# Holding the modulation steps of a two-layer RWKV/attention kernel behind VectorE's work on the tile in front, and ordering them by halves of c

## The chip, the cores and the metric

The kernel runs on one core of one Trainium2 chip. The metric is the device time of one execution in microseconds (us), the median of several runs. One further execution was taken with the hardware profiler; the views of the profile and of the trace quoted here are of that execution. TensorE is PE in them (PEld its weight loads), VectorE DVE, ScalarE ACT, GpSimd POOL, and SyncE, which issues most transfers, SP.

## The reference

A sequence of 256 positions with 2048 features passes an RWKV-7 layer and an attention layer, each followed by an MLP, all in fp32. Every normalised input is shifted and scaled, and every branch is gated, by vectors that come from one conditioning vector c ("modulation"):

```python
for layer in range(DEPTH):                      # DEPTH = 2
    mod = c @ w_ada[layer] + b_ada[layer]       # 2048 x 12288
    sh1, sc1, gt1, sh2, sc2, gt2 = jnp.split(mod, 6, axis=-1)
    if layer == N_A_LAYERS:
        sh_kv, sc_kv = jnp.split(c @ w_ada_kv + b_ada_kv, 2, axis=-1)
        h_kv = modulate(rms_norm(x, g_kv), sh_kv, sc_kv)
        k_s, v_s = h_kv @ w_k_shared, h_kv @ w_v_shared
    h = modulate(rms_norm(x, g_mix[layer]), sh1, sc1)
    y = rwkv7_time_mix(h, ...) if layer < N_A_LAYERS else chunk_band_attention(h, ...)
    x = x + gt1[:, None, :] * y
    h = modulate(rms_norm(x, g_mlp[layer]), sh2, sc2)
    x = x + gt2[:, None, :] * sq_relu_mlp(h, w_up[layer], w_down[layer])
return rms_norm(x, g_final)
```

## The kernel before, in words

The program passes these stages; the times are those of the trace of before.

| stage | us |
|---|---|
| first modulation vectors on TensorE, v projection | 0 to 190 |
| time mixing | 190 to 704 |
| out_proj with `w_o` | 704 to 797 |
| MLP 0: four quarters of 16 up tiles and 16 down tiles | 797 to 1556 |
| shared K (first 8 tiles to 1607, last 8 to 1653) | 1556 to 1653 |
| shared V: 16 tiles | 1653 to 1748 |
| q and the attention itself: 16 tiles | 1748 to 1882 |
| out_proj with `attn_w_o`: 16 tiles | 1882 to 1970 |
| MLP 1, as MLP 0 | 1970 to 2707 |

**A weight tile** comes in two halves of 128x1024. Each half is loaded into `raw` (six buffers, SP's queue), ScalarE rounds it to `wH` (L380), VectorE takes `wL = raw - wH` (L383), and TensorE multiplies by both parts (`proj2`, L414 and L415). There are three buffers of wH and wL, so TensorE has at most one and a half tiles ahead of it. VectorE then takes the result out of PSUM: `t`, `vf` or `q` at L934, `x` at L919 (the output projections) and L990 (the MLPs), and splits activations in two parts (`hHL` L965, `aHL` L543).

**A modulation step** handles one of 384 tiles of 512 KB of `w_ada_t`: VectorE multiplies the tile by a broadcast half of c (`cb`) and sums along the row (L461). A modulation vector ("key", such as (1, 4): layer 1, part 4) has 16 tiles for each half of c, 32 steps in all. Its two halves of sums are added at the end (L463 of the changed program, L466 to L469 of the one before), and the key is then in `ada_done`. The order is that of `ada_tiles`: key by key, both halves of a key in turn, the half that comes first alternating, so that c's half changes at every key's middle. `cb` has one buffer: a change waits for the last step with the old half, then loads 512 KB over SP. There are 13 such loads.

In the time mixing (steps 0 to 110) the tiles come through `raw`. Later they come through `rada` in an `ada_room`, by GpSimd's queue (L370): five buffers in MLP 0, three in the attention with its output projection, five in MLP 1. `ada_fill` asks for the next tiles as buffers come free. The program asks for steps 111 to 285 in MLP 0 (`ada_tick`: one and two by turns behind each tile), 286 to 293 in the second half of K (one a tile), 294 to 325 in V (two a tile), 326 to 347 beside q (one, and two at every third tile), 348 to 351 in the `ada_need` ahead of the attention's output projection (L610), 352 to 363 in that projection, and 364 to 383 in MLP 1. `ada_need` takes steps until the named keys are done: (1, 2) is the gate that the projection's x updates use, (1, 4) and (1, 3) are the scale and shift of the MLP behind it.

That is the order in which the program is written. A scheduler then orders the instructions of each engine by when their operands are ready, and may draw an instruction ahead of those written earlier, unless it is written in `tc.issue_after(instruction)`, which keeps it behind that instruction. The steps have no such mark.

Of the kernel before, what the change touches and what calls it, by code (L numbers as in the profile page):

```python
# [12 lines left out]
F32 = mybir.dt.float32  # L13
F32R = mybir.dt.float32r
AF = mybir.ActivationFunctionType
ALU = mybir.AluOpType
AX = mybir.AxisListType

P = 128
D = 2048  # L20
T = 256
KT = D // P
# [8 lines left out]
HK = 8  # L31
# [298 lines left out]
class Body:  # L330
# [96 lines left out]
        return tile_, self.bada[:, at:at + KT]  # L427

    def ada_tiles(self):
        for key in [(0, 2), (0, 4), (0, 3), (0, 5), ("kv", 1), ("kv", 0),  # L430
                    (1, 1), (1, 0), (1, 2), (1, 4), (1, 3), (1, 5)]:
            for last in range(2):
                for n in range(KT):
                    yield key, last, n

    def ada_load(self):
        tile_ = next(self.adas, None)
        if tile_ is not None:
            key, last, n = tile_
            if n == 0 and last:  # L440
                self.half = 1 - self.half
            raw = self.raw(self.d["w_ada_t"][self.ada_src(*key)[0] + n, self.half], ada=True)
            self.ada_q.append((key, last, n, raw))
        return tile_ is not None

    def c_half(self):
        n_ = HK * P
        self.cb = self.wp.tile([P, n_], F32, tag="cb", bufs=1, name="cb")
        self.nc.sync.dma_start(out=self.cb, in_=self.d["c_row"][0:1, self.cb_half * n_:(self.cb_half + 1) * n_].to_broadcast([P, n_]))
        self.cb_half = 1 - self.cb_half  # L450

    def ada_step(self):
        nc = self.nc
        if not (self.ada_q or self.ada_load()):
            return
        key, last, n, raw = self.ada_q.popleft()
        if self.cb is None:
            self.c_half()
        dst, bias = self.mods[key], self.ada_src(*key)[1]
        sums = dst if last else self.sums  # L460
        nc.vector.scalar_tensor_tensor(out=raw, in0=raw, scalar=1.0, in1=self.cb, op0=ALU.mult, op1=ALU.mult,  # L461
                                       accum_out=sums[:, n:n + 1])
        if n < KT - 1:  # L463
            return
        if last:
            nc.vector.tensor_tensor(out=dst, in0=dst, in1=self.sums, op=ALU.add)  # L466
            self.ada_done.add(key)
        else:
            nc.vector.tensor_tensor(out=self.sums, in0=self.sums, in1=bias, op=ALU.add)  # L469
            self.c_half()  # L470

    def ada_fill(self):
        while self.ada_pool and len(self.ada_q) < self.ada_pool[1] - 1 and self.ada_load():
# [5 lines left out]
            self.ada_step()  # L479

    def ada(self, n=1):
        for _ in range(n):
            self.ada_step()
        self.ada_fill()

    def last_pe(self):
        pe = self.nc.tensor.engine
        return next(i for i in reversed(self.nc.cur_bb.bb.instructions) if i.engine == pe)

    def ada_need(self, *keys):  # L490
        while not all(k in self.ada_done for k in keys):
# [74 lines left out]
    def run(self):  # L566
        nc, tc, d = self.nc, self.tc, self.d
        ctx = self.ctx
        gp = self.gp = ctx.enter_context(tc.tile_pool(name="gp", bufs=1))
        self.wp = ctx.enter_context(tc.tile_pool(name="wp", bufs=2))  # L570
        nc.scalar.preload_act_table_set("natural_log_exp_and_others")
        self.hp = ctx.enter_context(tc.tile_pool(name="hp", bufs=2))
        self.csts = gp.tile([P, CST.shape[1]], F32, name="csts")
        self.vecs = gp.tile([P, len(VECS), KT], F32, name="vecs")
        self.bada = gp.tile([P, 2 * 96 + 32], F32, name="bada")
        self.ct = gp.tile([P, KT], F32, name="ct")
        nc.scalar.dma_start(out=self.ct, in_=d["c"])
        self.mods = {}
        for layer in (0, 1, "kv"):
            for part in range(2 if layer == "kv" else 6):  # L580
                self.mods[(layer, part)] = gp.tile([P, KT], F32, name=f"mod_{layer}_{part}")
        self.nhalf, self.pool_every = 0, 0
        self.ada_pool, self.half, self.cb, self.cb_half = None, 0, None, 0
        self.sums = gp.tile([P, KT], F32, name="ada_sums")
        self.ada_done = set()
        self.adas, self.ada_q = self.ada_tiles(), deque()

        sv, sp = ExitStack(), ExitStack()
        v = self.layer_a(sv, sp)
        with ExitStack() as st:  # L590
            self.np = st.enter_context(tc.tile_pool(name="npl", bufs=1, side="right", reuse_waits="tile"))
            xp = st.enter_context(tc.tile_pool(name="xp", bufs=1, side="right", reuse_waits="tile"))
            self.x = xp.tile([P, KT, T], F32, name="x")
            for j in range(KT - 2, KT):
                self.split(self.y_hl, j, v[:, j, :])
            sv.close()
            self.ada_need((0, 2), (0, 4), (0, 3))
            nxt = self.out_proj(self.pp, "w_o", self.y_hl, (0, 2), "g_mlp0", (0, 4), (0, 3), self.o_ps)
            sp.close()
            with ExitStack() as s2:  # L600
                pp = s2.enter_context(tc.tile_pool(name="ps_m0", bufs=2, space=bass.MemoryType.PSUM, reuse_waits="tile"))
                self.psm = lambda: pp.tile([P, 512], F32, tag="m", bufs=2, name="m")
                s2.enter_context(self.ada_room(5))
                nxt = self.mlp(s2, pp, 0, *nxt, "g_kv", ("kv", 1), ("kv", 0))
            with ExitStack() as s2:
                pp = s2.enter_context(tc.tile_pool(name="ps_at", bufs=2, space=bass.MemoryType.PSUM, reuse_waits="tile"))
                self.psm = lambda: pp.tile([P, 512], F32, tag="m", bufs=1, name="m")
                s2.enter_context(self.ada_room(3))
                o_hl = self.attention(s2, pp, *nxt)
                self.ada_need((1, 2), (1, 4), (1, 3))  # L610
                nxt = self.out_proj(pp, "attn_w_o", o_hl, (1, 2), "g_mlp1", (1, 4), (1, 3))
            with ExitStack() as s2:
                pp = s2.enter_context(tc.tile_pool(name="ps_m1", bufs=2, space=bass.MemoryType.PSUM, reuse_waits="tile"))
                self.psm = lambda: pp.tile([P, 512], F32, tag="m", bufs=2, name="m")
                s2.enter_context(self.ada_room(5))
                self.mlp(s2, pp, 1, *nxt)
                r = self.rstd()
                for lo, hi, eng in ((0, 4, nc.vector), (11, 14, nc.gpsimd), (4, 8, nc.vector), (8, 11, nc.vector),
                                    (14, KT, nc.gpsimd)):
                    x = self.x[:, lo:hi, :]  # L620
                    eng.tensor_tensor(out=x, in0=x, in1=r.unsqueeze(1).to_broadcast([P, hi - lo, T]), op=ALU.mult)
                    (nc.sync if eng is nc.vector else nc.scalar).dma_start(out=d["out"][:, lo:hi, :], in_=x)
# [388 lines left out]
    def attention(self, st, pp, scaled, kv_gain, kv_shift):  # L1011
# [8 lines left out]
        def projected(src, hl, dst, ada, between=()):  # L1020

            between = iter(between)
            w = self.weight(src)
            ps = pp.tile([P, 2, T], F32, tag="pj", bufs=2, name="pj")
            for q in range(0, KT, 4):
                ins = self.proj2(ps, w, lambda kt: hl[:, kt, :, 0:T], (q, q + 4))
                with tc.issue_after(ins):
                    next(between, lambda: None)()
            self.sum2(dst, ps)
            self.ada(ada)  # L1030
# [171 lines left out]
```

## Time and profile before

| | us |
|---|---|
| runs | median of 3: 2716.94 (2716.22 to 2721.14) |
| profiled execution, device time | 2709.22 |
| its span in the profile | 2707.5 |
| PE busy | 2596.7 (96%) |
| VectorE busy | 2088.7 (77%) |
| ScalarE busy | 1334.1 (49%) |
| GpSimd busy | 350.2 (13%) |

In rows of the timeline the columns are start, duration, engine, line, operation, output<-input, shape, and in brackets the idle time ahead of it with what ended it. In rows of groups they are line, engine, operation, names, count, busy time and mean ns, idle time ahead with its releasers. In rows of waits: engine, tile and line, what it waited for, us in all, times, the longest. In rows of stretches: the stretch, its length, the busy time and count of each engine named in the text, the granted clock of TensorE, the DMA engines' share and GB/s. Consecutive VectorE instructions overlap a little, so a duration is slightly longer than the distance from start to start.

### The profile page before, as it was taken

To read this page: it belongs to the slowest core of one execution; us is meant where nothing else is said; L and a number is where in the kernel's file an instruction comes from. 1 tells how busy PE (TensorE), PEld (TensorE's weight loads), DVE (VectorE), ACT (ScalarE), POOL (GpSimd) and SP (SyncE) were. 2 spreads that over 40 slices of the span, in tenths; PEclk is the share of its full clock that TensorE was granted. 3 is DMA by queue.
4 is the path that set the end of the run, shared out by engine and by line. 5 is a ranking of instruction groups with operands and counts; after the bars stand their busy time and mean duration, and the time that the engine had idled before them with its cause. 6 is when DMAs were issued, how large, how long until landed. Compare 5 with 4: busy or idle time off the path is not lost.

```text
span 2707.5 us, 55672 instructions
## 1 busy us (share of the span) xinstructions
PE 2596.7 (96%) x22154; PEld 2215.5 (82%) x22154; DVE 2088.7 (77%) x3493; ACT 1334.1 (49%) x2432; POOL 350.2 (13%) x593
## 2 busy tenths in 40 slices
PE   6998999999999999999989999999999999999997
PEld 3777778777889888888877898877898888888886
DVE  5778888889699999999888884577985555555555
ACT  3345545555445445355345554465464464453553
POOL 0001322323121111121111100000200000000002
PEclk8999999999999999999999999999999999999998
DMA  9976656566698999999999655555855555555553
GB/s 334 314 236 210 201 187 199 192 200 225 236 323 307 370 365 380 383 382 357 354 349 336 231 197 184 184 172 196 289 190 188 187 189 186 188 187 187 188 187 117
DMA packets 219253, 669.28 MB, mean 247 GB/s; under 512 B 21616, under 2 KB 69104, under 8 KB 218992
## 3 DMA queue, kind: packets, MB, share of 16 engines
q1 hardware_dynamic: 173520, 516.36, 55.9%
q0 software_dynamic: 39312, 143.15, 14.4%
q10 hardware_dynamic: 6160, 6.21, 0.7%
q8 instruction: 174, 2.85, 0.4%
q14 instruction: 87, 0.71, 0.1%
HBM read 663.54 MB, written 2.10 MB: 246 GB/s over the span
## 4 chain that ended last, share of the span: by engine, by line
PE 63%; issue 13%; DVE 12%; DMA 6%; ACT 2%; POOL 2%; SPq 0%; DVEq 0%; POOLq 0%; ACTq 0%
PE pj L414 33%; PE pj L415 16%; DVE wL L383 4%; DMA raw<-w_ada_t 3%; DVE rada L461 2%; POOL rada L370 2%; DMA cb<-c_row 2%; PE pj L404 2%; PE pj L405 2%; PE pj L403 2%; DVE raw L461 1%; PE iv L111 1%; PE ms L324 1%; ACT wH L380 1%; DVE x L919 1%
## 5 line engine op out<-in xcount | busy, mean ns | idle before, releaser
L383 DVE TENSOR_TENSOR wL<-raw,wH 128x1024 fp32r<-128x1024 f32 x772 | 943.1, 1222 | 356.6 <-ACT wH L380 352.1
L414 PE MATMUL pj<-aHL,wH 128*128 128x512 f32 x3328 | 1207.9, 404 | 2.1 <-DVE x L919 1.2
L380 ACT CAST wH<-raw 128x1024 fp32r<-128x1024 f32 x772 | 803.7, 1043 | 720.8 <-PE pj L414 611.9
L415 PE MATMUL pj<-aHL,wL 128*128 128x256 f32 x3328 | 940.0, 282 | 16.6 <-DVE wL L383 15.9
L414 PEld LDWEIGHTS pj<-aHL,wH 128*128 128x128 f32 x3328 | 632.7, 190 | 156.1 <-issue 10.3
L414 PE MATMUL pj<-hHL,wH 128*128 128x512 f32 x2048 | 723.8, 399 | 4.1 <-DVE hHL L965 4.1
L415 PEld LDWEIGHTS pj<-aHL,wL 128*128 128x128 f32 x3328 | 632.6, 190 | 25.1 <-DVE wL L383 23.5
L415 PE MATMUL pj<-hHL,wL 128*128 128x256 f32 x2048 | 574.4, 281 | 5.7 <-DVE wL L383 5.7
L414 PEld LDWEIGHTS pj<-hHL,wH 128*128 128x128 f32 x2048 | 384.7, 188 | 100.4 <-DVE hHL L965 5.4
L415 PEld LDWEIGHTS pj<-hHL,wL 128*128 128x128 f32 x2048 | 386.7, 189 | 7.5 <-DVE wL L383 7.2
L461 DVE SCALAR_TENSOR_TENSOR rada<-rada,cb 128x1024 f32<-128x1024 f32 x273 | 331.2, 1217 | 49.0 <-DMA cb<-c_row 32.9
L370 POOL DMA_DIRECT2D rada<-w_ada_t x273 | 145.4, 533 | 682.0 <-DVE rada L461 636.1
L990 DVE SCALAR_TENSOR_TENSOR x<-pj,mod,x 128x256 f32<-128x256 f32 x256 | 123.2, 481 | 53.6 <-PE pj L415 50.7
L461 DVE SCALAR_TENSOR_TENSOR raw<-raw,cb 128x1024 f32<-128x1024 f32 x111 | 137.9, 1246 | 25.4 <-DMA raw<-w_ada_t 25.2
L511 POOL TENSOR_TENSOR ss<-ss,sq 128x256 f32<-128x256 f32 x56 | 50.9, 909 | 796.7 <-ACT sq L510 796.4
L962 ACT ACTIVATE t<-t 128x256 f32<-128x256 f32 x112 | 46.8, 418 | 194.2 <-DVE t L934 193.9
L405 PE MATMUL pj<-aHL,wL 128*128 128x258 f32 x384 | 108.8, 284 | 1.4 <-DVE wL L383 1.4
L404 PE MATMUL pj<-aHL,wH 128*128 128x258 f32 x384 | 109.7, 286 | 0.0
L403 PE MATMUL pj<-aHL,wH 128*128 128x258 f32 x384 | 109.5, 285 | 0.0
L405 PEld LDWEIGHTS pj<-aHL,wL 128*128 128x128 f32 x384 | 73.9, 193 | 2.1 <-DVE wL L383 2.1
L404 PEld LDWEIGHTS pj<-aHL,wH 128*128 128x128 f32 x384 | 73.3, 191 | 0.1
L403 PEld LDWEIGHTS pj<-aHL,wH 128*128 128x128 f32 x384 | 72.9, 190 | 0.2
(241 smaller groups left out, 2837.6 us busy)
## 6 DMA issues: line engine op xcount, KB each, us to landing
rada<-w_ada_t POOLq DMA_DIRECT2D x273, 512.0 KB, 6.3
raw<-w_up SPq DMA_DIRECT2D x256, 512.0 KB, 4.9
raw<-w_down SPq DMA_DIRECT2D x256, 512.0 KB, 4.8
raw<-w_ada_t SPq DMA_DIRECT2D x111, 512.0 KB, 4.4
rawa<-w_ada SPq DMA_DIRECT2D x64, 512.0 KB, 6.9
raw<-w_k SPq DMA_DIRECT2D x32, 512.0 KB, 3.7
raw<-w_r SPq DMA_DIRECT2D x32, 512.0 KB, 5.0
raw<-w_o SPq DMA_DIRECT2D x32, 512.0 KB, 5.4
```

Of the source, the lines that this page charges most:

```text
L370: queue.dma_start(out=t, in_=src)
L380: nc.scalar.copy(Hf, raw)
L383: eng.tensor_tensor(out=Lf, in0=raw, in1=Hf, op=ALU.subtract)
L403: nc.tensor.matmul(ps, H[:, i, :], a(kt)[:, 0, :], start=(first and kt == 0), stop=False)
L404: nc.tensor.matmul(ps, H[:, i, :], a(kt)[:, 1, :], start=False, stop=False)
L405: ins = nc.tensor.matmul(ps, L[:, i, :], a(kt)[:, 0, :], start=False, stop=(last and kt == KT - 1))
L414: nc.tensor.matmul(ps, H[:, i, :], a(kt), start=(kt == 0), stop=False)
L415: ins = nc.tensor.matmul(ps[:, 0, :], L[:, i, :], a(kt)[:, 0, :], start=False, stop=(kt == KT - 1))
L461: nc.vector.scalar_tensor_tensor(out=raw, in0=raw, scalar=1.0, in1=self.cb, op0=ALU.mult, op1=ALU.mult, accum_out=sums[:, n:n + 1])
L511: (eng or nc.gpsimd).tensor_tensor(out=self.ss, in0=self.ss, in1=sq, op=ALU.add)
L962: nc.scalar.activation(t, t, AF.Relu)
L990: nc.vector.scalar_tensor_tensor(out=x, in0=ps[:, i, :], scalar=self.mods[(layer, 5)][:, n:n + 1], in1=x, op0=ALU.mult, op1=ALU.add)
```

## The change

A step that is asked for in an `ada_room` through `ada` is now written in `issue_after(last VectorE instruction written so far)`. It stays behind VectorE's work on the tile in front of it. Steps that `ada_need` and `ada_drain` take call `ada_step` itself, and have no such mark. `ada_tiles` walks six runs of one half of c each, several keys long, so c's half changes five times: after steps 48, 112, 160, 224 and 320. The last run holds the second halves of (1, 2), (1, 4), (1, 3) and (1, 5): the first three of these keys end at steps 335, 351 and 367. Before, the fourth-last to second-last key ended at 287, 319 and 351. `cb` keeps one buffer; the half is loaded at the first step that needs it.

```diff
-        for key in [(0, 2), (0, 4), (0, 3), (0, 5), ("kv", 1), ("kv", 0),
-                    (1, 1), (1, 0), (1, 2), (1, 4), (1, 3), (1, 5)]:
-            for last in range(2):
+        a, b, c = (0, 2), (0, 4), (0, 3)
+        e, f, g = (0, 5), ("kv", 1), ("kv", 0)
+        rest = [(1, 1), (1, 0), (1, 2), (1, 4), (1, 3), (1, 5)]
+        runs = [(0, [a, b, c]), (1, [a, b, c, e]), (0, [e, f, g]), (1, [f, g] + rest[:2]), (0, rest), (1, rest[2:])]
+        seen = set()
+        for half, keys in runs:
+            for key in keys:
                 for n in range(KT):
-                    yield key, last, n
+                    yield key, half, n, key in seen
+                seen.add(key)
...
+        if self.cb_half != half:
+            n_, self.cb_half = HK * P, half
+            self.cb = self.wp.tile([P, n_], F32, tag="acc", bufs=1, name="cb")
+            nc.sync.dma_start(out=self.cb, in_=self.d["c_row"][0:1, half * n_:(half + 1) * n_].to_broadcast([P, n_]))
...
     def ada(self, n=1):
-        for _ in range(n):
-            self.ada_step()
+        nc = self.nc
+        with self.tc.issue_after(self.last_on(nc.vector)) if self.ada_pool else nullcontext():
+            for _ in range(n):
+                self.ada_step()
         self.ada_fill()
 
+    def last_on(self, eng):
+        return next(i for i in reversed(self.nc.cur_bb.bb.instructions) if i.engine == eng.engine)
```

How this moves VectorE's instructions is shown at three places. Lines from 489 on have a number smaller by one in the changed program. First, VectorE in the third quarter of MLP 0, down tiles 6 to 8; `x` is the tile's update, `wL` a weight half, `rada` a step, and `cb` the half of c. Before:

```order
L990 SCALAR_TENSOR_TENSOR x_10905<-pj_16501,mod_0_5_75,x_10905 128x256
L461 SCALAR_TENSOR_TENSOR rada_19919,ada_sums_84<-rada_19919,cb_17925 128x1024
L383 TENSOR_TENSOR wL_16601<-raw_16598,wH_16600 128x1024
L461 SCALAR_TENSOR_TENSOR rada_19975,ada_sums_84<-rada_19975,cb_17925 128x1024
L990 SCALAR_TENSOR_TENSOR x_10905<-pj_16551,mod_0_5_75,x_10905 128x256
L383 TENSOR_TENSOR wL_16645<-raw_16642,wH_16644 128x1024
L990 SCALAR_TENSOR_TENSOR x_10905<-pj_16551,mod_0_5_75,x_10905 128x256
L461 SCALAR_TENSOR_TENSOR rada_19977,ada_sums_84<-rada_19977,cb_17925 128x1024
L383 TENSOR_TENSOR wL_16651<-raw_16648,wH_16650 128x1024
L461 SCALAR_TENSOR_TENSOR rada_20033,ada_sums_84<-rada_20033,cb_17925 128x1024
```

And of the change:

```order
L383 TENSOR_TENSOR wL_16589<-raw_16586,wH_16588 128x1024
L383 TENSOR_TENSOR wL_16595<-raw_16592,wH_16594 128x1024
L989 SCALAR_TENSOR_TENSOR x_10901<-pj_16545,mod_0_5_75,x_10901 128x256 x2
L460 SCALAR_TENSOR_TENSOR rada_16428,ada_sums_84<-rada_16428,cb_16219 128x1024
L460 SCALAR_TENSOR_TENSOR rada_16479,ada_sums_84<-rada_16479,cb_16219 128x1024
L383 TENSOR_TENSOR wL_16639<-raw_16636,wH_16638 128x1024
L383 TENSOR_TENSOR wL_16645<-raw_16642,wH_16644 128x1024
L989 SCALAR_TENSOR_TENSOR x_10901<-pj_16598,mod_0_5_75,x_10901 128x256 x2
L460 SCALAR_TENSOR_TENSOR rada_16481,ada_sums_84<-rada_16481,cb_16219 128x1024
```

Two steps a tile, here with buffers (19919 to 20033) that the program asks for in V,, have become one and two by turns, each behind its own tile's x.

Second, VectorE in V, some tiles in the middle; `vf` is what is taken out of PSUM. Before:

```order
L934 TENSOR_TENSOR vf<-pj,vf 128x256
L383 TENSOR_TENSOR wL<-raw,wH 128x1024 x2
L934 TENSOR_TENSOR vf<-pj,vf 128x256
L383 TENSOR_TENSOR wL<-raw,wH 128x1024 x2
L934 TENSOR_TENSOR vf<-pj,vf 128x256
```

And of the change:

```order
L933 TENSOR_TENSOR vf<-pj,vf 128x256
L460 SCALAR_TENSOR_TENSOR rada,mod_3_79<-rada,cb 128x1024 x2
L383 TENSOR_TENSOR wL<-raw,wH 128x1024 x2
L933 TENSOR_TENSOR vf<-pj,vf 128x256
L460 SCALAR_TENSOR_TENSOR rada,mod_3_79<-rada,cb 128x1024 x2
L383 TENSOR_TENSOR wL<-raw,wH 128x1024 x2
```

Two steps stand now between a tile's result and the weight halves of a later tile, where there were none.

Third, VectorE at the start of the attention's output projection. `pj` of one number holds a tile's two partial results, each added to `x` by an L919 (L918), `gain_g_mlp1` is made from the key (1, 4), `aHL` is the scaled input of MLP 1. Before:

```order
L564 TENSOR_TENSOR aHL_20795<-po_22434,aHL_20795 128x256
L919 SCALAR_TENSOR_TENSOR x_10905<-pj_22465,mod_1_2_78,x_10905 128x256 x2
L383 TENSOR_TENSOR wL_22584<-raw_22581,wH_22583 128x1024
L383 TENSOR_TENSOR wL_22590<-raw_22587,wH_22589 128x1024
L543 SCALAR_TENSOR_TENSOR aHL_22557<-x_10905,gain_g_mlp1_22462,aHL_22557 128x256
L461 SCALAR_TENSOR_TENSOR rada_23347,ada_sums_84<-rada_23347,cb_21450 128x1024
L919 SCALAR_TENSOR_TENSOR x_10905<-pj_22510,mod_1_2_78,x_10905 128x256
L383 TENSOR_TENSOR wL_22629<-raw_22626,wH_22628 128x1024
L919 SCALAR_TENSOR_TENSOR x_10905<-pj_22510,mod_1_2_78,x_10905 128x256
```

And of the change:

```order
L463 TENSOR_TENSOR mod_1_4_80<-mod_1_4_80,ada_sums_84 128x16
L383 TENSOR_TENSOR wL_22557<-raw_22554,wH_22556 128x1024
L460 SCALAR_TENSOR_TENSOR rada_22450,ada_sums_84<-rada_22450,cb_20661 128x1024
L460 SCALAR_TENSOR_TENSOR rada_22453,ada_sums_84<-rada_22453,cb_20661 128x1024
L460 SCALAR_TENSOR_TENSOR rada_22456,ada_sums_84<-rada_22456,cb_20661 128x1024
L495 SCALAR_TENSOR_TENSOR gain_g_mlp1_22499<-mod_1_4_80,vecs_66 128x16
L918 SCALAR_TENSOR_TENSOR x_10901<-pj_22502,mod_1_2_78,x_10901 128x256
L383 TENSOR_TENSOR wL_22621<-raw_22618,wH_22620 128x1024
L460 SCALAR_TENSOR_TENSOR rada_22459,ada_sums_84<-rada_22459,cb_20661 128x1024
L918 SCALAR_TENSOR_TENSOR x_10901<-pj_22502,mod_1_2_78,x_10901 128x256
L460 SCALAR_TENSOR_TENSOR rada_22462,ada_sums_84<-rada_22462,cb_20661 128x1024
L542 SCALAR_TENSOR_TENSOR aHL_22594<-x_10901,gain_g_mlp1_22499,aHL_22594 128x256
```

The steps of the keys that `ada_need` asks for stand now among the x updates and weight halves of the projection's first tiles, one to three between two of them; before, none of those keys' steps was left here.

More of the change, by code (lines that the diff above doesn't have):

```diff
@@ L438, in ada_load @@
         if tile_ is not None:
[L439 to L443, printed above, removed]
-        return tile_ is not None
[L446 to L450, printed above, removed]
+            key, half, n, last = tile_
+            raw = self.raw(self.d["w_ada_t"][self.ada_src(*key)[0] + n, half], ada=True)
+            self.ada_q.append((tile_, raw))
+        return tile_ is not None
     def ada_step(self):
@@ L455, in ada_step @@
             return
-        key, last, n, raw = self.ada_q.popleft()
-        if self.cb is None:
-            self.c_half()
+        (key, half, n, last), raw = self.ada_q.popleft()
+        if self.cb_half != half:
+            n_, self.cb_half = HK * P, half
+            self.cb = self.wp.tile([P, n_], F32, tag="acc", bufs=1, name="cb")
+            nc.sync.dma_start(out=self.cb, in_=self.d["c_row"][0:1, half * n_:(half + 1) * n_].to_broadcast([P, n_]))
         dst, bias = self.mods[key], self.ada_src(*key)[1]
-        sums = dst if last else self.sums
+        sums = self.sums if last else dst
         nc.vector.scalar_tensor_tensor(out=raw, in0=raw, scalar=1.0, in1=self.cb, op0=ALU.mult, op1=ALU.mult,
                                        accum_out=sums[:, n:n + 1])
[L463 to L470, printed above, removed]
+        if n == KT - 1:
+            nc.vector.tensor_tensor(out=dst, in0=dst, in1=self.sums if last else bias, op=ALU.add)
+            if last:
+                self.ada_done.add(key)
     def ada_fill(self):
@@ L481, in ada @@
     def ada(self, n=1):
-        for _ in range(n):
-            self.ada_step()
+        nc = self.nc
+        with self.tc.issue_after(self.last_on(nc.vector)) if self.ada_pool else nullcontext():
+            for _ in range(n):
+                self.ada_step()
         self.ada_fill()
+    def last_on(self, eng):
+        return next(i for i in reversed(self.nc.cur_bb.bb.instructions) if i.engine == eng.engine)
     def last_pe(self):
-        pe = self.nc.tensor.engine
-        return next(i for i in reversed(self.nc.cur_bb.bb.instructions) if i.engine == pe)
+        return self.last_on(self.nc.tensor)
     def ada_need(self, *keys):
@@ L582, in run @@
         self.nhalf, self.pool_every = 0, 0
-        self.ada_pool, self.half, self.cb, self.cb_half = None, 0, None, 0
+        self.ada_pool, self.cb_half = None, None
         self.sums = gp.tile([P, KT], F32, name="ada_sums")
```

## The prediction

> **What bounds the kernel now.** I read the page first: the span, the busy shares, the costly groups.
>
> ```profile
> span 2707.5 us, 55672 instructions
> PE 2596.7 (96%) x22154; PEld 2215.5 (82%) x22154; DVE 2088.7 (77%) x3493; ACT 1334.1 (49%) x2432; POOL 350.2 (13%) x593
> L461 DVE SCALAR_TENSOR_TENSOR rada<-rada,cb 128x1024 f32<-128x1024 f32 x273 | 331.2, 1217 | 49.0 <-DMA cb<-c_row 32.9
> ```
>
> TensorE (PE) is busy 96% of the span, so only the 4% in which it waits can be won; any PE wait that is added costs its whole length. VectorE (DVE) runs the modulation steps (L461, 273 of them outside the time mixing). The second reading is the stretches: MLP 0, the second half of K, V, q with attention, and MLP 1, first for all work, then for the tile `rada` alone.
>
> ```profile
> 797.00:1556.00 759.00, 732.16 (x4207) 638.27 (x4208) 699.56 (x1074) 367.21 (x548) 136.27 (x250) 0.99 0.93 346
> 1607.00:1653.00 46.00, 46.00 (x265) 40.18 (x264) 31.25 (x47) 24.06 (x37) 0.00 (x0) 1.00 0.56 191
> 1653.00:1748.00 95.00, 95.00 (x555) 83.44 (x554) 45.32 (x50) 44.55 (x65) 0.00 (x0) 1.00 0.52 180
> 1748.00:1882.00 134.00, 133.64 (x854) 103.79 (x853) 102.58 (x255) 80.84 (x223) 8.94 (x59) 1.00 0.55 185
> 1970.00:2707.00 737.00, 721.61 (x4216) 633.05 (x4214) 437.48 (x564) 368.25 (x547) 20.51 (x16) 0.99 0.56 181
> ```
>
> ```profile
> 704.00:797.00 93.00, 15.40 (x25) 9.53 (x17) 1.00 0.80 283
> 797.00:1556.00 759.00, 293.19 (x482) 124.96 (x236) 0.99 0.93 346
> 1556.00:1882.00 326.00, 0.00 (x0) 2.66 (x5) 1.00 0.55 187
> 1882.00:1970.00 88.00, 24.61 (x40) 8.25 (x15) 1.00 0.79 272
> ```
>
> The columns after the length are the busy times of PE, PEld, DVE, ACT, POOL, then clock, DMA share and GB/s; the second table has DVE and POOL only. VectorE is busy 699.56 of 759 us in MLP 0. An L461 instruction and the read of its sum count as two there, so MLP 0 runs 241 steps. The program puts 175 steps in MLP 0 and 78 in the attention; the trace has none between 1556 and 1882. The scheduler has drawn them all forward into MLP 0, because a step waits for little but its load.
>
> What that costs is seen by comparing the two MLPs, which have the same matmuls. The lines are the x updates of both output projections and of both MLPs.
>
> ```profile
> L919 DVE SCALAR_TENSOR_TENSOR x<-pj,mod,x x16: 470/472/484, 752.1 to 795.9; 128x256 f32<-128x256 f32 x16
> L919 DVE SCALAR_TENSOR_TENSOR x<-pj,mod,x x32: 466/471/485, 1882.6 to 1969.0; 128x256 f32<-128x256 f32 x32
> L990 DVE SCALAR_TENSOR_TENSOR x<-pj,mod,x x128: 471/478/485, 898.0 to 1554.8; 128x256 f32<-128x256 f32 x128
> L990 DVE SCALAR_TENSOR_TENSOR x<-pj,mod,x x128: 482/484/486, 2066.2 to 2691.4; 128x256 f32<-128x256 f32 x128
> ```
>
> From the last L919 to the last L990: 1554.8−795.9 = 758.9 us in MLP 0, 2691.4−1969.0 = 722.4 us in MLP 1 (128 tiles, 5.64 us each). MLP 0 loses **36.5 us**. The waits in MLP 0 name the cause:
>
> ```profile
> DVE rada L461 <- DMA cb<-c_row: 28.4, 7, 4.7
> DVE rada L461 <- DMA rada<-w_ada_t: 15.8, 19, 3.1
> PE pj L415 <- DVE wL L383: 19.8, 12, 4.0
> PE pj L414 <- DVE hHL L965: 4.1, 3, 1.5
> ```
>
> VectorE waits for c's half 28.4 us and for step loads 15.8 us, and TensorE waits for VectorE's weight halves; a VectorE with 8% to spare can't make that good.
>
> **The change part by part.**
>
> *MLP 0.* It keeps 175 steps, one and two by turns behind each tile, instead of 241. By the rows below, start to start, a step takes 1.14 us of VectorE, an x update 0.40, half a weight tile 1.13 (with rounding 1.14).
>
> ```profile
> 1296.28 1.21 DVE L461 SCALAR_TENSOR_TENSOR rada<-rada,cb 128x1024 f32<-128x1024 f32 x1
> 1297.42 0.48 DVE L990 SCALAR_TENSOR_TENSOR x<-pj,mod,x 128x256 f32<-128x256 f32 x1
> 1297.82 1.21 DVE L383 TENSOR_TENSOR wL<-raw,wH 128x1024 fp32r<-128x1024 f32 x1
> 1298.95 0.47 DVE L990 SCALAR_TENSOR_TENSOR x<-pj,mod,x 128x256 f32<-128x256 f32 x1
> ...
> 1297.80 0.53 POOL L370 DMA_DIRECT2D rada<-w_ada_t  x1 [1.75 <-DVE rada L461]
> ```
>
> So 66×1.14 = 75 us of VectorE work go; 699.56−75 = 624 of 722 us is 86%. A tile with two steps needs 2×1.14+2×1.14+2×0.40 = 5.4 us, under the 5.64 of TensorE. Five buffers hold 3.3 tiles' steps, 18.8 us, longer than any load below. I take the whole **−36.5**. The 12 steps that ran among the last 8 tiles of w_o leave too: those tiles came at 43.8/7.5 = 5.84 us, attention's at 86.4/15.5 = 5.57, so **−2.0**.
>
> *c's halves.* In MLP 0 three changes remain. Each is dear:
>
> ```profile
> 1322.56 1.21 DVE L461 SCALAR_TENSOR_TENSOR rada<-rada,cb 128x1024 f32<-128x1024 f32 x1
> 1331.68 1.23 DVE L461 SCALAR_TENSOR_TENSOR rada<-rada,cb 128x1024 f32<-128x1024 f32 x1 [4.63 <-DMA cb<-c_row]
> ```
>
> From the old half's last step to the new half's first pass 9.12 us. In the new order about 3 us of other work lies between two steps, so VectorE may still stand 4.6 us; tiles waiting ahead of TensorE (one and a half of them in three halves of W) hide most. Bounds 0 and 4.6 each; I take 1: **+3**. In the time mixing two loads of c go; L461's waits there name no c, so 0.
>
> *K and V.* Eight steps of 1.14 in K's second half meet a VectorE that is free for 46.0−31.25 = 14.8 us there; bounds 0 and, if none of that cover fell right, 9: **+0.5**, near the cover. In V each tile now has two steps ahead of its weight halves. A V tile before:
>
> ```profile
> 1676.70 0.42 DVE L934 TENSOR_TENSOR vf<-pj,vf 128x256 f32<-128x256 f32 x1
> 1678.35 1.23 DVE L383 TENSOR_TENSOR wL<-raw,wH 128x1024 fp32r<-128x1024 f32 x1 [1.23 <-ACT wH L380]
> 1682.54 0.41 DVE L934 TENSOR_TENSOR vf<-pj,vf 128x256 f32<-128x256 f32 x1
> ```
>
> Tile pitch 5.84; work 2.6 plus 2.28 for two steps: it fits. But only three buffers serve here. The load into a buffer is issued 1297.80−1296.28 = 1.52 us after its step begins, and the step that uses it begins L later, L being the load's landing time. Walking the row "v a a w w" over two tiles, they can't be shorter than 1.52+L+1.14+2.28+0.33 = L+5.3: free up to L = 6.4, +5 us over 16 tiles at 7.0. The loads:
>
> ```profile
> DMA to landing us min/median/max: 4.5/6.4/8.4
> DMA to landing us min/median/max: 3.8/5.7/7.7
> ```
>
> The first line is 1268 to 1330 us (MLP 0 at its busiest), the second 1890 to 1960 (the nearest to what comes: beside an output projection's weights). Bounds for V 0 and 11 (L = 7.7); with the one change of c in it I take **+2**.
>
> One sentence of the Trainium skill bears on L: page "DMA: Bandwidth & Descriptors", section "Anatomy of one DMA — SWDGE (gpsimd) path", fits a transfer as 2.0 us plus its bytes over 436 GB/s, an estimate of 3.2 us for these 512 KB. The trace disagrees, its shortest being 3.8 in these stretches, since several transfers share the engines; by the page alone the terms that hang on L would come out below those of the first rival.
>
> *q.* A step or two beside each tile's scores. A tile before, from q to q 8.34 us:
>
> ```profile
> 1820.88 0.41 DVE L934 TENSOR_TENSOR q<-pj,q 128x256 f32<-128x256 f32 x1
> 1822.34 1.23 DVE L383 TENSOR_TENSOR wL<-raw,wH 128x1024 fp32r<-128x1024 f32 x1 [1.04 <-ACT wH L380]
> 1824.29 0.56 DVE L1074 SCALAR_TENSOR_TENSOR s<-S,s 128x384 f32<-128x384 f32 x1 [0.72 <-PE S L1073]
> ```
>
> One step fits in the 1.04 us gap; a second, taken in six of the 16 tiles, delays the softmax by 2.28−1.04−0.72 = 0.5 us, or by 1.2 if the first gap alone hides. Bounds 0 and 7; **+3**, from 0.5 a tile.
>
> *Attention's end.* This is the dear part. The steps for (1,2), (1,4), (1,3) now end at step 367, and 20 are left when `ada_need` asks for them (4 before). `ada_need` issues them unheld, and gain and x updates of the output projection wait for their sums. I walked VectorE's new row from q_14's eviction to the second weight half of out_proj's tile 5: 27 steps (30.8 us), 11 halves (12.5), 9 x (3.6), and the last scores and small work, 13: **60 us** of its own. (The 13 are an estimate: the stretch below has 12.41 of VectorE before the first x, less three halves 9.0; then four aHL of 0.4 and some 2.4 of waits for TensorE.) With three buffers each three steps also take 1.52+L, 7.5 at L = 6.0, against 60/9 = 6.7 of work: the waits sum to 17. Then TensorE finishes tile 5 (halves of 2.82 us) 82.0 us after q_14's eviction; the walk gives 71.5 at L = 4.6, 79.6 at 5.7, 90.0 at 7.0, 95.6 at 7.7. Before:
>
> ```profile
> 1862.56:1882.61 20.05, 19.96 (x120) 14.18 (x119) 12.41 (x34) 10.53 (x31) 2.89 (x7) 1.00 0.69 246
> ```
>
> ```profile
> 1862.56 0.41 DVE L934 TENSOR_TENSOR q<-pj,q 128x256 f32<-128x256 f32 x1
> 1912.77 0.47 DVE L919 SCALAR_TENSOR_TENSOR x<-pj,mod,x 128x256 f32<-128x256 f32 x1
> ```
>
> Tile 5's x came 50.2 us after it. So 82.0−50.2 = **+31.8**, with bounds +15 (no wait at all: 82−17) and +45. I take L = 6.0, a little over the median 5.7, since a row of three ends with its slowest. After tile 5 about one step a tile remains in out_proj and 4 in MLP 1: 0.
>
> *Sum.* −36.5−2.0+3+0.5+2+3+31.8 = **+1.8 us**. The profiled execution took 2709.22 us around its span of 2707.5; it lies 7.7 under the median of the runs, 2716.94, to which I carry the difference: 2718.7, say **2719**.
>
> **The rivals.**
>
> *The bunched loads are quick* (the other side: faster). With TensorE waiting, fewer weights are on their way, and L falls to 4.6. The end of attention then costs 71.5−50.2 = 21.3, V 1: −36.5−2+3+0.5+1+3+21.3 = −9.7, **2707**; without any wait for loads 15 in place of 21.3, 2701. It decides at L = 5.7, where the sum is zero. For it: the 3.8 minimum. Against: the median just there.
>
> *The loads are slow* (slower). At L = 7.0 the end costs 39.8, V 6: −35.5+0.5+6+3+39.8 = +13.8, **2731**; with q at its 7, 2735. For it: 6.4 median and 8.4 maximum where three buffers ran beside full weights.
>
> *MLP 0 is not healed* (the change does not do what it says): holding each step behind its tile makes VectorE's row stiffer, a late load then holds weight halves, and only four of seven waits for c go, 4/7×28.4 = 16 us. +1.8+36.5−16 = +22, **2739**. For it: 15.8 us of waits for loads already. Against: five buffers, 86%.
>
> **How the numbers follow.** Forecast 0.45 (0.24 within 0.2%, that is 5.4 us, about what a measurement of this kernel can tell from no change; 0.18 above, from the upper bounds of q, V and c; 0.03 below), quick loads 0.30, slow loads 0.15, MLP 0 unhealed 0.10. Faster 0.30+0.03 = 0.33, same 0.24, slower 0.18+0.15+0.10 = 0.43. The range reaches from below the 2701 of the first rival to above the 2739 of the third: 2699 to 2744.
>
> **What would show it.** Right: no wait of L461 for c beyond three in MLP 0, last L919 to last L990 near 725 us, V still at 5.84 a tile, and at attention's end PE waiting some 30 us for wL and x with L461 waiting for `rada`. Wrong: PE waits in MLP 0 over 10 us; V tiles over 6 us; or tile 5's x under 70 us after q_14's eviction.

## The result, and the profile after

The changed kernel takes 2706.16 us (median of 12 runs, 2692.70 to 2710.03) against 2715.28 for the one before (12 runs). The ratio is 0.9963, 95% interval 0.9948 to 0.9977: faster by 9 us or 0.37%, where a change of +1.8 us, to 2719, had been forecast. The profiled execution took 2708.89 us, only 0.3 less than the 2709.22 of the profiled execution of before; why is the first thing to read.

Three lines of the page of the change:

```profile
span 2707.1 us, 55697 instructions
PE 2596.2 (96%) x22154; PEld 2219.7 (82%) x22154; DVE 2098.1 (78%) x3493; ACT 1339.2 (49%) x2432; POOL 349.9 (13%) x593
L460 DVE SCALAR_TENSOR_TENSOR rada<-rada,cb 128x1024 f32<-128x1024 f32 x273 | 327.6, 1220 | 29.3 <-DMA rada<-w_ada_t 15.5
```

The totals hardly differ from before. L460's idle time fell from 49.0 to 29.3 us, and a load of a step, no longer c, is what ends most of it. Where the time went is told by the x updates, the ends of both output projections and both MLPs, of the change:

```profile
L918 DVE SCALAR_TENSOR_TENSOR x<-pj,mod,x x16: 471/484/485, 758.9 to 796.9; 128x256 f32<-128x256 f32 x16
L989 DVE SCALAR_TENSOR_TENSOR x<-pj,mod,x x128: 469/484/486, 899.1 to 1523.8; 128x256 f32<-128x256 f32 x128
L918 DVE SCALAR_TENSOR_TENSOR x<-pj,mod,x x32: 471/478/484, 1862.9 to 1968.8; 128x256 f32<-128x256 f32 x32
L989 DVE SCALAR_TENSOR_TENSOR x<-pj,mod,x x128: 482/484/487, 2066.0 to 2691.1; 128x256 f32<-128x256 f32 x128
```

The first row begins at 758.9 where before's begins at 752.1: 6.8 us are lost up to there, in stages whose work the change touches only by the order of the steps and by two loads of c fewer. From there w_o's last tiles take 38.0 us instead of 43.8. MLP 0, from 796.9 to 1523.8, takes 726.9 instead of 758.9. The last L918 is 0.2 us earlier than before's, so the 31 us won by 1523.8 are gone again at 1968.8. MLP 1 is as it was.

The stretches of the change: MLP 0, V, and the piece from q_14's eviction to tile 5's x, which carried the dearest term of the prediction; the last row is the same piece of before.

```profile
797.00:1525.00 728.00, 722.68 (x4237) 634.84 (x4236) 635.24 (x939) 370.90 (x550) 104.47 (x187) 1.00 0.88 313
1622.00:1718.00 96.00, 93.60 (x536) 81.86 (x536) 79.48 (x114) 42.78 (x63) 16.75 (x32) 0.98 0.94 341
1834.80:1913.56 78.76, 58.67 (x282) 45.59 (x281) 65.02 (x118) 26.93 (x52) 18.11 (x33) 0.85 0.80 271
```

```profile
1862.56:1912.77 50.21, 48.92 (x283) 39.03 (x282) 40.04 (x75) 25.65 (x51) 9.70 (x18) 1.00 0.76 264
```

VectorE's share in MLP 0 fell from 92% to 87% (635.24 of 728) and TensorE is busy for all but 5 us of it. In the last piece it is the other way round: VectorE has 65.02 us of work where it had 40.04, TensorE does the same 283 matmuls (one record is missing), and the piece is 28.6 us longer. The waits from 1824 to 1915 us, VectorE's first, then TensorE's:

```profile
DVE rada L460 <- DMA rada<-w_ada_t: 10.4, 10, 2.1
DVE mx L1080 <- ACT s L1078: 1.7, 4, 0.7
DVE aHL L563 <- ACT aHL L562: 1.1, 1, 1.1
DVE wL L383 <- ACT wH L380: 0.7, 1, 0.7
DVE s L1073 <- issue: 0.3, 1, 0.3
```

```profile
PE pj L414 <- DVE x L918: 13.3, 4, 4.4
PE pj L415 <- DVE wL L383: 4.0, 3, 2.4
PE pT L1093 <- DVE s L1082: 2.8, 2, 1.7
```

TensorE's waits are not the whole of the 28.6 us: its matmuls took 58.67 us where they took 48.92, at a granted clock of 0.85 instead of 1.00. The slower clock is still not what makes the piece long. VectorE works for 65.02 us of the 78.76 and waits for the steps' loads for 10.4, and its list has no wait for TensorE, so about 3 us are left in which anything else could hold it up.

A new wait stands in the list: TensorE's next tile (L414) waits four times for an x update (L918), which takes an earlier tile out of PSUM, and the x update stands behind forced steps, that is steps that `ada_need` takes. Six rows of the timeline show it at tiles 2 and 3, two of the steps waiting for their loads:

```profile
1883.79 1.23 DVE L460 SCALAR_TENSOR_TENSOR rada<-rada,cb 128x1024 f32<-128x1024 f32 x1
...
1886.35 1.23 DVE L460 SCALAR_TENSOR_TENSOR rada<-rada,cb 128x1024 f32<-128x1024 f32 x1 [1.33 <-DMA rada<-w_ada_t]
...
1887.50 0.48 DVE L918 SCALAR_TENSOR_TENSOR x<-pj,mod,x 128x256 f32<-128x256 f32 x1
1890.08 1.23 DVE L460 SCALAR_TENSOR_TENSOR rada<-rada,cb 128x1024 f32<-128x1024 f32 x1 [2.10 <-DMA rada<-w_ada_t]
...
1891.22 0.87 DVE L918 SCALAR_TENSOR_TENSOR x<-pj,mod,x 128x256 f32<-128x256 f32 x2
1892.01 1.22 DVE L460 SCALAR_TENSOR_TENSOR rada<-rada,cb 128x1024 f32<-128x1024 f32 x1
```

### The profile page after: what moved, and what is told of

Its sections match the earlier page's. It is cut to its first block, busy times and chain, and to the rows that moved or that the text cites. A ratio compares the mean times of both kernels' runs of the same rounds, so it can differ in the third digit from the quotient of the medians.

```text
span 2707.1 us, 55697 instructions
## 1 busy us (share of the span) xinstructions
PE 2596.2 (96%) x22154; PEld 2219.7 (82%) x22154; DVE 2098.1 (78%) x3493; ACT 1339.2 (49%) x2432; POOL 349.9 (13%) x593
## 4 chain that ended last, share of the span: by engine, by line
PE 71%; DVE 7%; issue 7%; DMA 6%; ACT 2%; POOL 1%; DVEq 0%; POOLq 0%; ACTq 0%; SPq 0%
PE pj L414 39%; PE pj L415 20%; DMA raw<-w_ada_t 3%; DVE wL L383 2%; PE pj L404 2%; PE pj L403 2%; PE pj L405 2%; DVE raw L460 1%; DMA rada<-w_ada_t 1%; DVE rada L460 1%; DMA cb<-c_row 1%; POOL rada L370 1%; PE iv L111 1%; PE ms L324 1%; ACT wH L380 1%
## 5 line engine op out<-in xcount | busy, mean ns | idle before, releaser
L414 PE MATMUL pj<-aHL,wH 128*128 128x512 f32 x3328 | 1211.5, 405 | 14.2 <-DVE x L918 13.3
L414 PEld LDWEIGHTS pj<-aHL,wH 128*128 128x128 f32 x3328 | 634.8, 191 | 170.3 <-issue 23.3
L414 PE MATMUL pj<-hHL,wH 128*128 128x512 f32 x2048 | 721.1, 397 | 1.6 <-DVE hHL L964 1.5
L414 PEld LDWEIGHTS pj<-hHL,wH 128*128 128x128 f32 x2048 | 384.4, 188 | 95.8 <-DVE hHL L964 2.2
L460 DVE SCALAR_TENSOR_TENSOR rada<-rada,cb 128x1024 f32<-128x1024 f32 x273 | 327.6, 1220 | 29.3 <-DMA rada<-w_ada_t 15.5
L460 DVE SCALAR_TENSOR_TENSOR raw<-raw,cb 128x1024 f32<-128x1024 f32 x111 | 138.1, 1249 | 29.2 <-DMA raw<-w_ada_t 28.1
```

The costliest lines, as they stand in the source:

```text
L414: nc.tensor.matmul(ps, H[:, i, :], a(kt), start=(kt == 0), stop=False)
```

## The experiments

The theory (A): holding the steps heals MLP 0; the order of keys, which leaves 20 steps to be forced where the attention ends, takes most of it back. Rivals: c's changes are the cause in MLP 0, and the hold itself is dear at the attention's end. The ratios below are to runs of the kernel before on the same chip; the stage times come from profiles on several chips. The stages are read from the same VectorE rows as above: up to w_o's first L919 or its like ("to w_o"), w_o's last tiles, MLP 0, K to q_14's eviction, from there to tile 5's x ("end"), to the last x of the projection, and MLP 1. Each row is one profiled execution (us), and the text compares with the first row unless it says otherwise:

| kernel | to w_o | w_o | MLP 0 | K, V, q | end | rest | MLP 1 | ratio to before (95%) |
|---|---|---|---|---|---|---|---|---|
| before | 752.1 | 43.9 | 758.8 | 307.8 | 50.2 | 56.3 | 722.3 | |
| before, again | 758.0 | 45.1 | 755.3 | 307.8 | 52.6 | 56.2 | 720.8 | |
| the change | 758.9 | 38.0 | 726.9 | 311.0 | 78.8 | 55.2 | 722.4 | 0.9963 (0.9948 to 0.9977) |
| the change, again | 754.6 | 38.0 | 726.8 | 309.7 | 77.2 | 55.2 | 720.8 | 0.9970 (0.9958 to 0.9983) |
| hold only | 753.2 | 39.3 | 740.7 | 312.7 | 51.4 | 55.2 | 730.6 | 0.9968 (0.9956 to 0.9981) |
| hold only, both c | 763.6 | 39.8 | 727.3 | 314.9 | 51.7 | 55.2 | 726.6 | 0.9898 (0.9881 to 0.9914) |
| order only | 749.5 | 43.8 | 746.5 | 307.6 | 46.4 | 56.6 | 720.8 | 0.9940 (0.9925 to 0.9954) |
| (1, 5) last | 757.2 | 38.6 | 731.1 | 310.6 | 51.7 | 55.2 | 732.7 | 0.9917 (0.9897 to 0.9938) |
| 18 steps without loads | 748.6 | 38.9 | 727.7 | 309.4 | 69.6 | 54.8 | 722.4 | 0.9927 (0.9908 to 0.9946) |
| 1.75 a tile | 753.6 | 39.4 | 730.3 | 309.4 | 47.7 | 55.2 | 722.5 | 0.9875 (0.9855 to 0.9895) |
| 1.75 a tile, both c | 762.6 | 39.8 | 724.6 | 313.2 | 47.8 | 55.2 | 722.4 | 0.9868 (0.9849 to 0.9887) |
| 1.75 a tile, one in q | 758.6 | 39.5 | 732.1 | 309.2 | 47.5 | 55.2 | 720.8 | 0.9888 (0.9871 to 0.9905) |

**Both kernels once more.** No edit.

> The changed kernel as it stands, with a second profile. The profiled execution of it ran out of step with its own median: 2708.89 us against 2706.16, and its time mixing was 7 us longer than before's. Theory A (the 7 us in the time mixing are chance): time mixing within 2 us of before's 190 to 704, total about 2702. Theory B (the new order of the steps costs the time mixing 7 us always): 7 us again, total about 2708 in the profiled execution. Both: MLP 0 -32, attention's end +27, q +4.

> The kernel before again, for a second profile of it. Theory A: the time mixing differs between two executions of one program by several us (the changed kernel's two differed by 4.8), while MLP 0 stays within 3 us of 745.3 (from the first held tile on). Rival: MLP 0 with its full VectorE is what scatters, by 5 us or more, and the time mixing is the same.

The change took 2702.49 us against 2710.39 (12 and 23 runs), 0.9970. "To w_o" it took 754.6, and before's second execution 758.0: two executions of one program differ there by 4.3 and 5.9 us, in opposite directions. Theory A of both expectations holds for the time mixing; MLP 0 of before also differs, by 3.5, so a difference of 3 us between two single profiles of it says little. Over all rows "to w_o" scatters from 748.6 to 763.6. The two longest are those with both halves of c in memory, but these two executions took 9.7 and 5.2 us more than the medians of their kernels, so no order by kernel is shown. From w_o on, the executions agree better: 1939.3 and 1937.9 before, 1932.2 and 1927.8 after, so the change is worth 6 to 12 us, as the medians say. The 6.8 us of the first profile lie within this scatter, whose cause stays open.

**The hold alone.** The edit, on the kernel before:

```diff
     def ada(self, n=1):
-        for _ in range(n):
-            self.ada_step()
+        with self.tc.issue_after(self.last_on(nc.vector)) if self.ada_pool else nullcontext():
+            for _ in range(n):
+                self.ada_step()
```

> Before, with the steps held behind VectorE's work on the tile in front, and nothing else: order of keys and 13 loads of c as before. Theory A (the hold heals MLP 0; the dear end of the attention comes from the order of keys alone, which leaves 20 steps for the need of the three keys): MLP 0 -30 (two or three more changes of c than in the full change cost 1 us each), q +4, attention's end 0, sum about -26, ratio 0.990. Rival (the hold itself costs at attention's end, and c's changes cost VectorE's full 4.6 us each): sum -5 to +5, ratio 1.000.

2701.50 against 2710.39: −9, not the −26 of theory A. The end fell as expected, to 51.4. Two other places took most of the difference. MLP 0 won 18 instead of 32, and its waits name c six times:

```profile
DVE rada L461 <- DMA cb<-c_row: 22.6, 6, 4.9
DVE rada L461 <- DMA rada<-w_ada_t: 1.5, 2, 1.4
PE pj L415 <- DVE wL L383: 13.2, 8, 3.0
```

And MLP 1 lost 8.2: 20 of the 32 steps of the key (1, 5) are left over there, where the change has 4, and those still open when the first down tiles need the key are forced among the weight halves.

**The hold alone, without c's changes in the MLPs.** The halves of c both stay in memory there (four buffers of steps for five); the edit's core:

```diff
+            if n == 5:
+                self.cbs = {self.now_half: self.cb, 1 - self.now_half: self.c_load(pool, 1 - self.now_half)}
...
+        if self.now_half != self.cb_half:
+            self.cb = self.cbs[self.cb_half] if self.cbs else self.c_load(self.wp, self.cb_half)
```

> The hold alone, with the old order of keys, and both halves of c held in the chip's memory in the MLPs (four buffers of steps instead of five there): the six changes of c in MLP 0 cost no load. Theory A (with the hold, six changes are what MLP 0 still loses: 13.2 us of waits of TensorE for weight halves): MLP 0 falls by 10 to 14 us against the hold alone, to the full change's MLP 0; total 12 to 15 under the hold alone, ratio 0.992. Rival (the old order loses for another reason, the places at which the keys end): within 4 us of the hold alone, ratio 0.996.

MLP 0 fell from 740.7 to 727.3, the change's own 726.9, and the waits for c are gone (one load waits, TensorE 2.8 us for weight halves):

```profile
DVE rada L467 <- DMA rada<-w_ada_t: 3.4, 1, 3.4
PE pj L426 <- DVE wL L394: 2.8, 4, 1.7
```

MLP 1 fell by 4.0 as well. Theory A holds: behind held steps, in the old order, six changes cost 13.4 us, 2.2 each. That price does not carry over to the change itself: in its MLP 0, with three changes, TensorE waits for weight halves 3.7 us in all (4 waits), at most 1.2 for each change, where the prediction had 1.

**The order alone.** The edit, on the change:

```diff
-        with self.tc.issue_after(self.last_on(nc.vector)) if self.ada_pool else nullcontext():
-            for _ in range(n):
-                self.ada_step()
+        for _ in range(n):
+            self.ada_step()
```

> The change without the hold: the new order of keys, five changes of c, but the scheduler free to draw steps forward. Theory A: VectorE in MLP 0 stays overfull, only the waits for c shrink from seven to three; -5 to -12 in MLP 0, nothing in V, q and attention's end; ratio 0.996 to 0.998. Rival (the waits for c are what MLP 0 loses): -25 or more, ratio 0.990.

2694.88: −15.5 or 0.9940, below the expected 0.996 to 0.998, and better than the whole change. MLP 0 won 12.3 us, the end 3.9. The stretch and the waits of MLP 0 (VectorE):

```profile
794.00:1540.00 746.00, 727.90 (x4200) 636.33 (x4201) 713.06 (x1106) 368.05 (x547) 145.89 (x266) 0.99 0.96 360
```

```profile
DVE rada L460 <- DMA rada<-w_ada_t: 16.0, 20, 1.9
DVE rada L460 <- DMA cb<-c_row: 11.9, 3, 4.9
```

VectorE is busy 713.06 of 746 us, fuller than before: still more steps are drawn forward. The waits for its loads are the 16 us they were, those for c 11.9 instead of 28.4. MLP 0 won 12.3 us, or 8.8 against before's second execution, so in an overfull engine half or more of a wait that is taken away is won, if the gain is put down to c alone. The rival that c is all of it falls, since 24 us over MLP 1's 722.3 remain, most of which the hold removes.

**The dear end.** First, fewer forced steps; (1, 5) goes last in both halves:

```diff
-        ... (0, rest), (1, rest[2:])]
+        ... (0, rest[:5]), (1, rest[2:]), (0, rest[5:])]
```

> The change with the key (1, 5) moved to the end in both halves, for one more change of c, so that the three keys are done 16 steps sooner and the need takes 4 steps instead of 20. Theory A (the +27 at attention's end are the 16 more forced steps): the end falls to 0 to +3, sum -29 to -32 against before, about 20 us or more under the change; ratio 0.988 to 0.990. Rival (the end is dear because held steps of the last q tiles and three buffers collide there, forced or not): at least 15 of the 27 us stay, ratio 0.993 or more.

2687.34, −23 or 0.9917. The end fell from 78.8 to 51.7: theory A. The waits of TensorE over the whole end and projection have no x among them any more:

```profile
PE pT L1093 <- DVE s L1082: 1.7, 1, 1.7
PE po L1100 <- ACT sT L1095: 0.2, 1, 0.2
```

A cost moved in, though: MLP 1 takes 732.7, because (1, 5) now ends late and its need forces steps among the weight halves of the first quarter's last up tiles, ahead of the first down tile (its x is at 2052.7 us, the last step at 2049.2). TensorE's waits in MLP 1:

```profile
PE pj L415 <- DVE wL L383: 6.8, 3, 3.5
PE m L515 <- DVE ss L510: 2.1, 1, 2.1
PE pj L414 <- DVE hHL L964: 1.4, 1, 1.4
PE pj L414 <- ACT wH L380: 0.8, 1, 0.8
```

Second, the change with 18 of its 20 forced steps without their loads, so that these 18 tiles of the modulation are left out of the computation:

```diff
+                self.kept = self.ada_q[-1][1]
                 self.ada_need((1, 2), (1, 4), (1, 3))
...
-            raw = self.raw(self.d["w_ada_t"][self.ada_src(*key)[0] + n, half], ada=True)
+            raw = self.kept or self.raw(self.d["w_ada_t"][self.ada_src(*key)[0] + n, half], ada=True)
```

> The change, but of the 20 steps that are forced at the attention's end 18 load nothing: they multiply c's half by itself, scaled by 0.001, into the last buffer, with the same instruction and shape. These 18 tiles of the modulation are left out of the computation. Theory A (two thirds of the dear end is VectorE's own work on the forced steps, one third their loads: the trace of the change has 10.4 us of waits for loads there): the end falls from +26 to +12 to +17. Rival (the loads, three at a time, are what the end waits for): it falls by 20 or more. Other rival (the loads hide behind the work): it stays within 4 us.

The end is 69.6, 19.4 over before's, instead of 28.6: 9.2 us belong to the loads, a third, and two thirds to VectorE's own work. That is theory A's share, and a fall of 9.2 us is at the low edge of its 9 to 14 (from +26 to between +12 and +17). Both rivals fall: one had 20 or more, the other less than 4. The waits there:

```profile
DVE rada L461 <- DMA rada<-w_ada_t: 2.1, 2, 1.6
PE pj L415 <- DVE wL L383: 6.6, 3, 3.7
PE pj L414 <- DVE x L921: 5.2, 2, 2.9
```

**A version that beats both.** More steps in MLP 0, so that none is forced later:

```diff
-        self.nticks = getattr(self, "nticks", 0) + 10
+        self.nticks = getattr(self, "nticks", 0) + 15
```

> The change with 1.75 instead of 1.5 steps behind each tile of the MLPs (the tick adds 15 instead of 10), so that MLP 0 takes some 26 steps more and no step is left for the needs ahead of the output projection and of MLP 1's down tiles. Theory A (26 us of the change are given back where ada_need forces steps at the attention's end): MLP 0 loses 2 to 4 us against the change, the attention's end falls by 26, MLP 1 stays without a wait: about 22 us under the change, ratio to before 0.987 to 0.990. Rival (VectorE in MLP 0 gets overfull again at 1.75 a tile): MLP 0 gives back 15 or more, ratio 0.993 or more.

2678.15 against 2713.72, 0.9875. MLP 0 runs 201 steps instead of 175 and gave back 3.4 us, the end is 47.7, MLP 1 has no step and no loss. The stretch of MLP 0 in it (1524 is 0.7 us past its end) shows that VectorE has room: 660.94 of 730 us.

```profile
794.00:1524.00 730.00, 720.48 (x4226) 632.67 (x4225) 660.94 (x992) 368.02 (x548) 116.52 (x213) 1.00 0.91 330
```

> The same, and in the MLPs both halves of c are held in the chip's memory, with four buffers of steps instead of five: three changes of c cost no wait in MLP 0. Theory A (a change of c behind held steps costs TensorE 1 to 2 us, the waits of the change's MLP 0 being 3.7 us for three): 2 to 5 us under the run with 1.75 steps alone. Rival (they are free, because TensorE has tiles ahead): equal to it within 2 us.

0.9868, an interval that covers the former. MLP 0 fell by 5.7 us against the run with 1.75 alone, but K, V and q took 3.8 more; by the total the two cannot be told apart.

> 1.75 steps behind each tile of the MLPs, and one step beside each tile of q where the change has two at every third. Theory A (the change's 5 to 8 us in V and q come from the second step of six tiles): the q stage is within 1 us of before's 126.9 us and the first q tiles too; against the run with 1.75 alone -2, ratio to before 0.9865. Rival (V's end and q lose by c's change and by any step at all): as the run with 1.75 alone.

The edit, beside the 15 of the tick, is `1` in place of `1 + (j % 3 == 0)` at the q tiles. The ratio is 0.9888, and K, V and q take 309.2 against 309.4: the rival holds. The second step costs nothing measurable; what the K, V and q stages lose, 1.4 us here, is not due to it.

## Why the prediction was wrong

The mechanism was right at most places, and so was the order of size of the largest terms; but the sum of +1.8 us is a small difference of large terms, and most were sized a few us too dear in the same direction. From the first row of w_o on the change was worth −7.1 us (first execution) and −11.5 (second), both against before's first execution. The steps that failed are the waits for loads at the attention's end, the second steps in q, and the pitch of w_o's tiles.

- **The end of the attention: +31.8 forecast, +28.6 and +27.0 measured, and a further −1.1 behind tile 5.** The landing time L failed here. It was set at 6.0 us "a little over the median 5.7". The landing times from 1837 to 1925 us in the change, and from 1830 to 1915 in its second execution, are:

```profile
DMA to landing us min/median/max: 3.8/5.0/7.5
```

```profile
DMA to landing us min/median/max: 3.8/4.7/7.5
```

  The waits for the loads were 10.4 and 9.5 us instead of the 17 of the walk; the walk's 60 us of VectorE's own work was too little (65.02 busy), which took most of that error back. TensorE waited 17.3 us for x and wL, not "some 30": most of the rest of its loss is slower matmuls at the lower clock. The Trainium skill, page "DMA: Bandwidth & Descriptors", section "Anatomy of one DMA — SWDGE (gpsimd) path", would give an estimate of 3.2 us for such a load alone; the trace's median of 5.0 is half as much again, in a stretch with 271 GB/s in all.
- **K, V and q: +5.5 forecast, +3.2 and +1.9 measured.** K costs nothing. V keeps its pitch of 5.84 us but for one tile of 10.12 us near its end, where c changes: from its first to its last result it takes 91.8 us, 4.2 more than 15 pitches before (2.3 more in the second execution), where +2 was forecast.

```profile
L933 DVE TENSOR_TENSOR vf<-pj,vf x16: 416/418/418, 1622.4 to 1714.2; 128x256 f32<-128x256 f32 x16
DVE rada L460 <- DMA cb<-c_row: 5.1, 1, 5.1
PE pj L415 <- DVE wL L383: 2.4, 1, 2.4
```

  In q the +3 for six second steps failed by its cause: up to q_14 the stage is 1.0 us shorter than before (0.8 in the second execution), and "one in q" shows nothing for the second step.
- **w_o's last tiles: −2.0 forecast, −5.8 measured.** The division of the stretch failed. Before's 43.8 us were taken as 7.5 tiles of 5.84 us, but the x updates of the first two tiles come 4 us apart, behind other work of VectorE. The six tiles behind them took 39.3 us, 6.55 each; in the change they took 33.4 us, 5.57 each, the pitch that the prediction had set. "Order only", where steps still run there, has 43.8; every held kernel 38.0 to 39.8.
- **MLP 0: −36.5+3 = −33.5 forecast, −31.9 and −32.0 measured** (−28.4 and −28.5 against before's second execution). Right in the mechanism, and in size within the scatter. The border to w_o is blurred: before, TensorE begins MLP 0 at 791.0 us, 4.9 ahead of w_o's last x. Both stages together were forecast at −35.5 and measured at −37.8 and −37.9 (−35.5 and −35.6 against before's second execution).
- **MLP 1 and time mixing: 0 forecast.** MLP 1 was right. The time mixing showed +6.8 in the first profile, which is within the scatter.

The rivals: "quick loads" gave 2707 and the time was 2706.16, and its landing time, 4.6, is near the 4.7 to 5.0 measured. That its number fits is luck: its end of 21.3 was not met. At L = 5.0 the walk gives about 74 us (between its 71.5 at 4.6 and 79.6 at 5.7), and 78.8 was measured. "Slow loads" and "MLP 0 not healed" fell. What the prediction did not weigh is how its two halves work against each other: "order only" costs nothing at the end, since a scheduler that is free draws the late keys' steps forward (257 steps in its MLP 0); with the hold they can't be drawn, and the late keys of the new order become a cost. The hold alone meets a different cost, six changes of c and a late (1, 5). Each half alone is worth at least as much as both (0.9968 and 0.9940 against 0.9963 and 0.9970).

## What to carry to other kernels

When work is pinned to its place, ask at each point that needs its result how much of it is left: that the scheduler drew steps forward had hidden it, and here a forced rest cost VectorE's whole time for it plus waits for its loads. Then look at the rate before the order: 1.75 instead of 1.5 steps a tile, one number, took away both forced places and made the gain three times as large. (It was tried with the new order only.) And where a forecast is the small rest of terms of 30 us, each error of 10% is the size of the answer, so the sign should be left open.

## What the runs showed of the hardware

- Between executions of one program the first stages, up to w_o's first x, differed by up to 6 us, and over kernels that share this work by 15 (748.6 to 763.6). One profile against one profile would have given −0.3 us for a change that is worth −9. The granted clock goes with it: its mean over the first 748 us was 0.98 in the three shortest (748.6, 749.5 and 752.1), 0.97 in eight and 0.96 in one of 762.6. Whether the clock makes the time, or waits make both, no run here shows.
- In the dear end the granted clock was 0.85 (1.00 in the same piece of before), beside waits of TensorE of up to 4.4 us; without the 18 loads it was 0.90 with a longest wait of 3.7:

```profile
1824.60:1894.20 69.60, 55.38 (x286) 43.53 (x285) 64.40 (x118) 26.96 (x52) 9.01 (x15) 0.90 0.50 171
```

  The Trainium skill, page "TensorE: Matmul & The Clock Gate", section "HAM oscillation — how this bites in real kernels", says that idle gaps over about 3.4 us halve the clock; these two rows agree with it, as far as a mean over the piece can show. V of the change does not fit as simply: the clock was 0.98 there, 0.86 from 1700 to 1712 us, beside a single wait of 2.4 us. That the lower clock cost little at the end is read from VectorE's row, which has no wait for TensorE; no run tried it.
